# mLSTM output product ahead of the gated unit, head normalisation in its own lane, one output-gate pair by seven products

## The chip, the cores and the metric

One NeuronCore of a Trainium2 chip runs the whole kernel. The metric is the device time of one execution in microseconds (us), shown as the median of several runs; a profiled execution gives the trace.

## The reference

One decoder layer over 1024 tokens and 16 meta tokens, D = 1024, float32. The parts that matter here:

```
p     = h @ w_in + b_in            # u_s5 | q | k | v | o | i | f | g_s5 | g_m
y_s5  = GLU(GELU(S5(u_s5)))        # S5: grouped state-space mixer; GLU by s5_w_glu (512 x 2048)
hm    = HeadNorm(mLSTM(q, k, v, i, f))            # 4 heads, value width 256
y_m   = (sigmoid(o) * hm) @ m_w_out               # 1024 x 1024
mix   = sigmoid(g_s5) * y_s5 + sigmoid(g_m) * y_m
h     = LN(alpha * h + mix @ w_o)
h     = LN(alpha * h + relu(h @ w_up + b_up)^2 @ w_down)
```

HeadNorm subtracts the mean and divides by the standard deviation over each head's 256 values.

## The kernel before, in words

Every large product is done in three matmuls: each operand is split into a high and a low part (`hi`, an fp32r copy made by ScalarE, and `lo`, the remainder made by VectorE), and `mm3` (L262 to L278) adds hi·hi, hi·lo and lo·hi in PSUM. A product with 512 columns and eight blocks of 128 rows is 24 matmuls.

The first half of the kernel is a list of jobs, written out by hand in `ORDER`. `q`, `v`, `u` and `o` jobs are projections of one weight tile each; an `o` job computes the output-gate tile `f` (two halves of 512 positions, eight blocks, three matmuls: 48 matmuls, `o_job`), applies the sigmoid and stores the row to `sig_dr`. An `a` and a `b` job together compute a *pair* of gate tiles by a Strassen scheme, with seven block products instead of eight, 12 matmuls each: `a` does products 1, 3 and 2, and stores weight sums (`gw_dr`) and a partial result (`e_dr`) for later; `b` does 6, 5, 7 and 4, where 4 is done in the next `b` job. For `b` the transformed activations `T` have replaced the activations in `hT_hi` and `hT_lo`. Pairs 0 to 3 are output-gate tiles 0 to 7 (tiles 2p and 2p+1), pairs 4 to 11 the gates g_s5 and g_m. The first three `b` jobs of the list keep their operands in SBUF (`HELD`); the others load them again. The last three `a` jobs are the `TAIL`, whose products are interleaved.

After the `b` jobs come eight `glu` jobs (48 matmuls each), eight `ym` jobs (48 each), and, outside the list, w_o, the up and the down products. Each job's weights are loaded two jobs ahead and split one job ahead (`job.after`).

Everything else runs in *lanes*: Python generators that `pump` advances while `mm3` emits matmuls. A lane's `yield d` lets it rest for d times its `PACE`, on a clock that counts a 512-column matmul as 0.2133 us. `ml` is the mLSTM recurrence, one chunk of 128 positions after the other (`A(c)`, `B(c)`), and with it the head normalisation `N(half, ...)`: a square root on ScalarE, short steps and four scalings on VectorE, eight transposes on TensorE, a copy on ScalarE. `s5c`, `s5` and `s5g` are the S5 tables, batches and GELU rows. `hg` (`hm_gate`) loads normalised rows and sigmoid rows, multiplies and stores them to `hm_dr`; `hmo_load` loads them again and splits them for `ym`, three in slots, five in rows of `hT`. `ah` and `up` prepare w_o and the up product. Loads and stores are issued on SP's queue in program order. The framework (`schedule_with_timeline_sim`) orders the instructions of each engine by a timeline of its own, so instructions of several jobs and lanes mix.

Of the kernel before, what the change touches and what calls it, by code (L numbers as in the profile page):

```python
# [16 lines left out]
D = 1024  # L17
# [20 lines left out]
LN2_1 = 0.693359375  # L38
LN2_2 = math.log(2.0) - LN2_1
MAGIC = 1.5 * 2 ** 23  # L40
ORDER = 'q1 q0 v0 v1 q3 q2 o3 v2 o6 o0 u0 u1 v3 o2 o7 o4 o5 u2 a4 o1 a6 u3 a5 a8 a7 a11 a9 a10 b11 b9 b10 b5 b8 b4 b6 b7'
HMO_AT = 4
HS = 3
HOLD = 3
TF = 1
TFA = 1
TLA = 1
T_UP = 0
REST = 17.25
G_E = [9]  # L50
G_L = [9, 10]
HGD = 1
UPD = 1
TPW = 5.95
S5_START = 'o3'
LANE_AT = {'t_prep': 'q1', 'hm_gate': 'b10', 'ah_scale': 'glu2', 'up_early': 'ym3'}
PACE = {'ml': 0.448, 'cv': 0.104, 's5': 1.05, 's5c': 0.683, 's5g': 2.31, 'ah': 0.834, 'up': 1.036, 'hg': 2.056}
UP = {'ml': 0, 'cv': 0, 's5': 0, 's5c': 0, 's5g': 0, 'ah': 0, 'up': 0, 'hg': 0}
SPLIT_UP = 0
PRE = 3  # L60
UP_AT = (0, 1, 4, 6)
ZD = 1
ML = [1.438, 1.186, 1.852, 10.348]
NL = [0.292, 2.192, 5.096, 3.406]
B5 = [16, 0.1, 0.1, 50]
C5 = [0.84, 0.84, 1.345, 1.05]
K5 = [1.18, 1.0, 8.0, 0.95]
Z5 = [2.284, 1.33, 1.336, 0.283]
D5 = [3.696, 1.28, 1.716, 0.267]
W5 = [5.284, 0.829, 10.595, 0.808]  # L70
Y5 = [0.959, 2.294, 4.502, 2.394]
CV0 = 0
HRA = 0
# [72 lines left out]
def decoder_block(  # L146
# [354 lines left out]
    def mlstm(h):  # L501
# [94 lines left out]
        for c in range(NCH):  # L596
            if c + 1 < NCH:
                A(c + 1)
            yield ML[h]
            B(c)  # L600
            yield ML[h]
            if c == 5:
                yield from N(0, nrm[0])
        yield 1.5
        yield from N(1, nrm[1])

    us_dr = dram.tile([512, 8, NB], F32, name="us_dr")
    ys_dr = dram.tile([4, P, 8, P], F32, name="ys_dr")
# [286 lines left out]
    def s5_batch(b):  # L895
# [71 lines left out]
        nc.sync.dma_start(ys_dr[b].rearrange("p g c -> p (g c)"), Y[:, 0:1024])  # L967
        lanes["s5g"].add(s5_gelu(b))

    def s5_gelu(b):  # L970
        yield 3.0
        yc = slot("s5yc")
        for g in range(8):
            src = ys_dr[b, :, (g % 2) * 4 + g // 2, :].rearrange("(t h) c -> h t c", h=16)
            nc.sync.dma_start(yc[16 * g:16 * g + 16, 0:1024].rearrange("p (t c) -> p t c", t=8), src)
        yield 14.0
        gf = slot("gelf")
        a_.activation(gf[:, 0:1024].rearrange("p (c t) -> p t c", t=8),
                      yc[:, 0:1024].rearrange("p (t c) -> p t c", t=8), AF.Gelu_apprx_tanh)
        hi, lo = slot("gelh", F32R), slot("gell", F32R)  # L980
        a_.activation(hi[:, 0:1024], gf[:, 0:1024], AF.Copy)
        v_.tensor_tensor(lo[:, 0:1024], gf[:, 0:1024], f32(hi[:, 0:1024]), op=OP.subtract)
        GEL[b] = (hi, lo)
        yield 2.6

    HMO = {}

    def hm_gate():
        rs = {}
        for f in range(KT + HGD):  # L990
            if f < KT:
# [12 lines left out]
    def hmo_load():
        rs = {}
        for k in range(KT + 2):
            if k < KT:
                rs[k] = slot("hmr")
                nc.sync.dma_start(rs[k][:, :D], hm_dr[k])
            if k >= 2:  # L1010
                r, q = rs.pop(k - 2), k - 2
                if q < HS:
                    HMO[q] = split_act(r, "hmo")
                else:
                    HMO[q] = hi, lo = hT_hi[:, q, 0:D], hT_lo[:, q, 0:D]
                    a_.activation(hi, r[:, :D], AF.Copy)
                    v_.tensor_tensor(lo, r[:, :D], f32(hi), op=OP.subtract)
            yield 1.2

    def split_act(src, name, n=1024):  # L1020
        hi, lo = slot(name + "h", F32R), slot(name + "l", F32R)
# [16 lines left out]

    MIX, SG, SGM = {}, {}, {}

    def sg_fetch(f):
        SG[f] = slot("sgs")
        nc.sync.dma_start(SG[f][:, :D], sig_dr[KT + f])

    def glu_job(f):
        def run(job):
            if f == 0:
                lanes["s5c"].drain()
                lanes["s5"].drain()
                lanes["s5g"].drain()  # L1050
                lanes["hg"].drain()
                sg_fetch(0)
            if f == HMO_AT:
                lanes["s5"].add(hmo_load())
            if f + 1 < KT:
                sg_fetch(f + 1)
            if f >= KT - 2:
                ms_fetch(f - KT + 2)
            (wh, wl), = job.w
            z2 = slot("z2s")  # L1060
            MIX[f] = SG.pop(f)
# [12 lines left out]
            if f == 0:  # L1074
                for zz in (1, 0):
                    for bi in range(2):
                        part(zz, bi, (0, 1, 2))
            for zz in (1, 0):
                for bi, (c0, c1) in enumerate(HALF):
                    part(zz, bi, (3,) if f == 0 else (0, 1, 2, 3))  # L1080
                    ps = pss[zz, bi]
                    if zz:
                        a_.activation(z2[:, c0:c1], ps, AF.Sigmoid)
                        if bi == 0:
                            job.after()
# [188 lines left out]
    def gb_job(p):  # L1274
        def run(job):
            last = list(GB)
            GB[p] = dict(w=job.w, e=job.w.pop("e") or HELD[p][2])
            if not B_AFT:
                job.after()
            gb_step(p, 6)  # L1280
            if B_AFT:
                job.after()
            gb_step(p, 5)
            for q in last:
                gb_step(q, 4)
# [215 lines left out]
    for w in ORDER.split():  # L1501
# [58 lines left out]
    for i, j in enumerate(jobs):  # L1560
# [610 lines left out]
```

## Time and profile before

| | us |
|---|---|
| median of 3 runs (lowest, highest) | 1501.3 (1501.07, 1501.62) |
| the profiled execution | 1501.45 |
| its span, first to last instruction | 1499.7 |
| TensorE busy | 1483.9 |
| VectorE busy | 1059.4 |
| ScalarE busy | 633.8 |

Busy times are of the profiled execution; matmuls overlap, and their ends are modelled, so busy TensorE time says when the engine had work and not how fast it ran.

### The profile page before, as it was taken

Reading aid. Unit: us, or ns where it says so; the run is one execution under the profiler, and the core shown is the slowest. Engines: PE = TensorE matmul, PEld = TensorE weight load, DVE = VectorE, ACT = ScalarE, POOL = GpSimd, SP = SyncE. Lnnn points to the kernel's source line nnn. Section 1 sums busy time; section 2 is a strip of 40 time slices with the busy share of each in tenths; the row PEclk is TensorE's granted clock in tenths of the full one; section 3 lists DMA queues with packets and bytes.
Section 4 is the critical chain, followed back from the end, with each engine's and each line's share of the span. In section 5 each row is a group of like instructions: output and inputs, shape, how many; then the busy total and the mean of one; then the engine's idle time right before and its main releaser. Section 6 shows DMA issues by size and latency. Waiting matters only on the chain.

```text
span 1499.7 us, 20533 instructions
## 1 busy us (share of the span) xinstructions
PE 1483.9 (99%) x7534; PEld 1253.1 (84%) x7534; DVE 1059.4 (71%) x1920; ACT 633.8 (42%) x1001; POOL 22.4 (1%) x113
## 2 busy tenths in 40 slices
PE   9999999999999999999999999999999999999997
PEld 9999888998888878888888888888888888888886
DVE  8875779686586765674786666566666789657786
ACT  7523544342366554231362244444444624333440
POOL 0000000000000000000000010000000000000000
PEclk9999999999999999999999999999999999999999
DMA  8544035647569699897782267444443997666652
GB/s 333 204 151 137 24 112 201 208 153 254 165 248 315 193 319 385 330 413 272 285 304 85 85 187 258 165 148 151 144 154 125 323 398 250 224 230 229 214 182 99
DMA packets 130516, 324.49 MB, mean 216 GB/s; under 512 B 18336, under 2 KB 32736, under 8 KB 130416
## 3 DMA queue, kind: packets, MB, share of 16 engines
q1 hardware_dynamic: 127392, 312.18, 59.4%
q0 software_dynamic: 3024, 11.01, 2.4%
q8 instruction: 59, 0.97, 0.3%
q14 instruction: 41, 0.34, 0.1%
HBM read 213.33 MB, written 109.81 MB: 215 GB/s over the span
## 4 chain that ended last, share of the span: by engine, by line
PE 82%; DVE 3%; ACT 2%; DMA 1%; issue 1%; SPq 0%; DVEq 0%; ACTq 0%
PE mm L276 20%; PE mm L274 20%; PE mm L275 20%; PE sd L276 6%; PE sd L275 6%; PE sd L274 6%; PE pn L542 1%; PE pn L543 1%; PE pu L546 1%; PE ln L1652 0%; DMA s5RS<-rr_dr 0%; PE s5y L962 0%; DVE s5w L935 0%; PE pS L532 0%; DMA s5yc<-ys_dr 0%
## 5 line engine op out<-in xcount | busy, mean ns | idle before, releaser
L274 PE MATMUL mm<-hT_hi,whi 128*128 128x512 f32 (+3 forms) x400 | 146.6, 367 | 0.0
L275 PE MATMUL mm<-hT_lo,whi 128*128 128x512 f32 (+3 forms) x400 | 146.2, 365 | 0.0
L276 PE MATMUL mm<-hT_hi,wlo 128*128 128x512 f32 (+3 forms) x400 | 145.5, 365 | 0.3 <-DVE wlo L255 0.3
L276 PE MATMUL sd<-dwh,dal 128*128 128x512 f32 (+1 forms) x256 | 99.1, 387 | 0.0
L275 PE MATMUL sd<-dwl,dah 128*128 128x512 f32 (+1 forms) x256 | 99.0, 387 | 0.0
L274 PE MATMUL sd<-dwh,dah 128*128 128x512 f32 (+1 forms) x256 | 98.6, 386 | 0.0
L1861 ACT ACTIVATE dah<-da 128x1024 fp32r<-128x1024 f32 x56 | 58.7, 1052 | 85.4 <-DMA da<-act_dr 36.2
L1865 ACT ACTIVATE dwh<-wdr 128x1024 fp32r<-128x1024 f32 x56 | 58.9, 1054 | 81.8 <-DVE wdr L1847 23.8
L276 PEld LDWEIGHTS mm<-hT_hi,wlo 128*128 128x128 f32 x400 | 75.3, 188 | 10.5 <-issue 0.7
L274 PEld LDWEIGHTS mm<-hT_hi,whi 128*128 128x128 f32 x400 | 75.3, 188 | 9.5 <-issue 0.5
L275 PEld LDWEIGHTS mm<-hT_lo,whi 128*128 128x128 f32 x400 | 75.3, 188 | 9.1 <-issue 0.3
L1862 DVE TENSOR_TENSOR dal<-da,dah 128x1024 fp32r<-128x1024 f32 x56 | 68.1, 1220 | 17.5 <-ACT dah L1861 17.4
L274 PE MATMUL mm<-dwh,dah 128*128 128x512 f32 (+1 forms) x208 | 79.8, 384 | 0.0
L276 PE MATMUL mm<-dwh,dal 128*128 128x512 f32 (+1 forms) x208 | 79.8, 385 | 0.0
L275 PE MATMUL mm<-dwl,dah 128*128 128x512 f32 (+1 forms) x208 | 79.7, 385 | 0.0
L274 PE MATMUL mm<-hT_hi,gmwh 128*128 128x512 f32 x192 | 76.9, 401 | 0.2 <-DVE gme L1255 0.2
L1866 DVE TENSOR_TENSOR dwl<-wdr,dwh 128x1024 fp32r<-128x1024 f32 x56 | 68.2, 1220 | 11.9 <-ACT dwh L1865 11.3
L275 PE MATMUL mm<-hT_lo,gmwh 128*128 128x512 f32 x192 | 75.7, 394 | 0.0
L276 PE MATMUL mm<-hT_hi,gmwl 128*128 128x512 f32 x192 | 74.6, 395 | 0.0
L274 PE MATMUL mm<-whi,hT_hi 128*128 128x256 f32 (+1 forms) x256 | 74.0, 290 | 0.0
L275 PE MATMUL mm<-wlo,hT_hi 128*128 128x256 f32 (+1 forms) x256 | 73.6, 288 | 0.0
L276 PE MATMUL mm<-whi,hT_lo 128*128 128x256 f32 (+1 forms) x256 | 73.2, 287 | 0.0
(468 smaller groups left out, 3843.7 us busy)
## 6 DMA issues: line engine op xcount, KB each, us to landing
da<-act_dr SPq DMA_DIRECT2D x56, 512.0 KB
wdr<-in_wdn_dram SPq DMA_DIRECT2D x56, 512.0 KB
wraw<-in_wf_dram SPq DMA_DIRECT2D x36, 512.0 KB
wur<-in_wup_dram SPq DMA_DIRECT2D x32, 512.0 KB
act_dr<-upy SPq DMA_DIRECT2D x64, 256.0 KB
wu_dr<-wpre SPq DMA_DIRECT2D x21, 512.0 KB
wpre<-wu_dr POOLq DMA_DIRECT2D x21, 512.0 KB, 5.3
act_dr<-upx SPq DMA_DIRECT2D x32, 256.0 KB
```

Source lines behind the costliest of these rows:

```text
L274: t_.matmul(ps, ah, bh, start=(i == 0 and part[0]), stop=False, skip_group_check=skip)
L275: t_.matmul(ps, ah, bl, start=False, stop=False, skip_group_check=skip)
L276: t_.matmul(ps, al, bh, start=False, stop=(i == n - 1 and part[1]), skip_group_check=skip)
L542: t_.matmul(pn[:, :258], qi[:, c0:c0 + n], Cs[c][:, :258], start=True, stop=False)
L543: t_.matmul(pn[:, :258], sws[c], vt[c][:, :258], start=False, stop=True)
L546: t_.matmul(pu[:, :258], kws[c][:n], vt[c][:n, :258], start=True, stop=True)
L1861: a_.activation(ah[:, :D], a[:, :D], AF.Copy)
L1862: v_.tensor_tensor(alo[:, :D], a[:, :D], f32(ah[:, :D]), op=OP.subtract)
L1865: a_.activation(wh, raw[i], AF.Copy)
L1866: v_.tensor_tensor(wl, raw[i], f32(wh), op=OP.subtract)
```

## The change

- `ORDER` is new. Jobs `o6` and `o7` are gone; pair 3 (`a3`, `b3`) computes these two gate tiles. `a3` stands after `v2`, where `o6` was; `b3` stands sixth among the nine `b` jobs. `a9 a5 a10` are the tail. Tiles 6 and 7 count as done (`OD`) after product 4 of pair 3, in the job after `b3`.
- The `ym` jobs come ahead of the `glu` jobs. `ym` stores sigmoid times product to `mix_dr`; `glu` loads it and adds. `hmo_load` has a lane `hm` that starts at the last `b` job and waits for gated rows and for free rows of `hT`. Up to three GELU rows go into rows of `hT`.
- `N` is added to a lane `hn` instead of being run inside `ml`, its first half after chunk 4 instead of 5. `HRA = 1` does two of four scalings on ScalarE.
- Paces, start points, priorities (`UP`, `T_UP`) and rests have new values.

```diff
-ORDER = 'q1 q0 v0 v1 q3 q2 o3 v2 o6 o0 u0 u1 v3 o2 o7 o4 o5 u2 a4 o1 a6 u3 a5 a8 a7 a11 a9 a10 b11 b9 b10 b5 b8 b4 b6 b7'
-HMO_AT = 4
+ORDER = 'q1 q0 v0 v1 q3 q2 o3 v2 a3 o0 u0 u1 v3 o2 o4 o5 u2 o1 a4 a6 a7 u3 a11 a8 a9 a5 a10 b9 b10 b5 b4 b3 b6 b8 b11 b7'
 HS = 3
+GH = 3
-T_UP = 0
-REST = 17.25
-G_E = [9]
-G_L = [9, 10]
+T_UP = 100
+REST = 11.83
+G_E = [5, 10]
+G_L = [5]
-LANE_AT = {'t_prep': 'q1', 'hm_gate': 'b10', 'ah_scale': 'glu2', 'up_early': 'ym3'}
-PACE = {'ml': 0.448, 'cv': 0.104, 's5': 1.05, 's5c': 0.683, 's5g': 2.31, 'ah': 0.834, 'up': 1.036, 'hg': 2.056}
+LANE_AT = {'t_prep': 'q0', 'hm_gate': 'a8', 'hmo': 'b7', 'ah_scale': 'ym5', 'up_early': 'glu3'}
+PACE = {'ml': 0.56, 'cv': 0.104, 's5': 1.103, 's5c': 0.683, 's5g': 3.512, 'ah': 1.602, 'up': 1.036, 'hg': 1.92, 'hn': 1.0, 'hm': 0.66}
+UP = {'ml': 10, 'cv': 0, 's5': 0, 's5c': 0, 's5g': 0, 'ah': 0, 'up': 0, 'hg': 0, 'hn': 0, 'hm': 0}
-ML = [1.438, 1.186, 1.852, 10.348]
-NL = [0.292, 2.192, 5.096, 3.406]
+ML = [1.912, 1.186, 1.815, 10.865]
+NL = [0.584, 3.726, 10.192, 11.252]
...
-HRA = 0
+HRA = 1
@@ mlstm @@
-            if c == 5:
-                yield from N(0, nrm[0])
-        yield 1.5
-        yield from N(1, nrm[1])
+            if c == 4:
+                lanes["hn"].add(N(0, nrm[0]))
+        lanes["hn"].add(N(1, nrm[1]))
@@ s5_gelu @@
-        GEL[b] = (hi, lo)
+        if 1 in ROWS and len(GROW) < GH:
+            GROW.append(KT - 1 - len(GROW))
+            GEL[b] = split_row(gf, GROW[-1])
+        else:
+            GEL[b] = split_act(gf, "gel")
@@ hm_gate @@
                 nc.sync.dma_start(hm_dr[f - HGD], a[:, :D])
+                GATED.add(f - HGD)
@@ hmo_load @@
             if k < KT:
+                while k not in GATED:
+                    yield 0.5
...
+                    while (q - HS) // 4 not in ROWS:
+                        yield 0.5
+                    HMO[q] = split_row(r, q - HS)
+    def split_row(src, row):
+        hi, lo = hT_hi[:, row, 0:D], hT_lo[:, row, 0:D]
+        a_.activation(hi, src[:, :D], AF.Copy)
+        v_.tensor_tensor(lo, src[:, :D], f32(hi), op=OP.subtract)
+        return hi, lo
@@ glu_job @@
-                        v_.tensor_tensor(MIX[f][:, c0:c1], z2[:, c0:c1], MIX[f][:, c0:c1], op=OP.mult)
-                        if bi == 1:
-                            nc.sync.dma_start(mix_dr[f], MIX.pop(f)[:, :D])
+                        v_.tensor_tensor(z2[:, c0:c1], z2[:, c0:c1], SG[f][:, c0:c1], op=OP.mult)
+                        v_.tensor_tensor(MIX[f][:, c0:c1], MIX[f][:, c0:c1], z2[:, c0:c1], op=OP.add)
@@ gb_job @@
             gb_step(p, 5)
+            if p == B_END:
+                ROWS.add(0)
...
             if p == B_END:
                 gb_flush()
+                ROWS.add(1)
@@ ym_job @@
-            lanes["s5"].drain()
+            if f == 0:
+                for n in ("cv", "ml", "hn", "hg", "hm"):
+                    lanes[n].drain()
+            if f + 1 < KT:
+                sm_fetch(f + 1)
+            if f >= KT - 2:
+                ms_fetch(f - KT + 2)
...
-                v_.tensor_tensor(MIX[f][:, c0:c1], MIX[f][:, c0:c1], SGM[f][:, c0:c1], op=OP.add)
...
+            nc.sync.dma_start(mix_dr[f], SGM.pop(f)[:, :D])
```

## Rows read from the trace of the kernel before

**Rows 1.** The page: span, busy time by engine, the chain that ended last.
```profile
span 1499.7 us, 20533 instructions
PE 1483.9 (99%) x7534; PEld 1253.1 (84%) x7534; DVE 1059.4 (71%) x1920; ACT 633.8 (42%) x1001; POOL 22.4 (1%) x113
PE 82%; DVE 3%; ACT 2%; DMA 1%; issue 1%; SPq 0%; DVEq 0%; ACTq 0%
```
**Rows 2.** Busy time by stretches (stretch, length, engines with counts, clock, DMA share, GB/s).
```profile
0.00:100.00 100.00, 97.10 (x782) 94.47 (x783) 83.26 (x178) 54.77 (x113) 3.33 (x42) 1.00 0.67 247
100.00:550.00 450.00, 445.37 (x2608) 391.28 (x2607) 323.47 (x794) 208.25 (x330) 7.33 (x49) 1.00 0.57 188
200.00:250.00 50.00, 49.23 (x319) 44.79 (x319) 46.56 (x155) 21.59 (x34) 2.05 (x17) 1.00 0.37 121
450.00:550.00 100.00, 99.25 (x467) 81.49 (x466) 71.39 (x113) 61.43 (x83) 0.95 (x1) 1.00 0.81 271
550.00:1450.00 900.00, 900.00 (x3923) 731.65 (x3922) 615.47 (x861) 368.36 (x551) 11.27 (x21) 1.00 0.66 234
1450.00:1499.70 49.70, 41.39 (x226) 35.73 (x224) 37.17 (x89) 2.38 (x8) 0.52 (x1) 0.96 0.23 85
```
**Rows 3.** Timeline of TensorE in a full stretch: start, length, instruction.
```profile
581.73 0.39 PE L276 MATMUL mm<-hT_hi,gmwl 128*128 128x512 f32 x1
...
586.84 0.39 PE L274 MATMUL mm<-gelh,whi 128*128 128x512 f32 x1
```
**Rows 4.** Waits of TensorE from 100 to 560 us: total, times, longest.
```profile
PE pt L586 <- DVE hraw L579: 1.8, 1, 1.8
PE pS L532 <- ACT kw L529: 0.7, 2, 0.5
PE s5y L962 <- DVE s5w L947: 0.6, 1, 0.6
PE pS L532 <- ACT hmF L587: 0.5, 1, 0.5
PE pn L542 <- DVE hmv L566: 0.3, 1, 0.3
PE mm L276 <- DVE wlo L255: 0.3, 1, 0.3
PE mm L274 <- DVE gme L1255: 0.2, 1, 0.2
```
**Rows 5.** Groups by line: busy us, mean ns, idle before, releaser.
```profile
L1462 DVE TENSOR_TENSOR wus<-wus,wraw 128x512 f32<-128x512 f32 x8 | 5.5, 687 | 0.2
L1023 DVE TENSOR_TENSOR gmwl<-wraw,gmwh 128x1024 fp32r<-128x1024 f32 x7 | 8.6, 1222 | 4.2 <-ACT gmwh L1022 4.2
L1022 ACT ACTIVATE gmwh<-wraw 128x1024 fp32r<-128x1024 f32 x8 | 8.5, 1062 | 4.3 <-DMA gw_dr<-wus 3.2 <-DMA gw_dr<-wraw 1.1
L564 ACT ACTIVATE hraw<-pn,dd 128x256 f32<-128x256 f32 x32 | 15.1, 473 | 71.2 <-DVE dd L563 64.2 <-PE pn L543 3.2 <-DVE cpre L356 2.6
L579 DVE TENSOR_SCALAR hraw<-hraw,hmv,hny 128x256 f32<-128x256 f32 x32 | 11.0, 408 | 0.0
```
**Rows 6.** Busy time by stretches: ten microseconds with the DMA engines full.
```profile
560.00:570.00 10.00, 10.00 (x45) 8.13 (x44) 6.27 (x7) 4.84 (x6) 0.00 (x0) 1.00 1.03 399
```
**Rows 7.** Timeline around the wait of the transposes.
```profile
148.67 1.28 ACT L207 ACT_TABLE_LOAD   x1
149.96 0.30 ACT L207 ACTIVATE hny<-hmv,eps_t 128x4 f32<-128x4 f32 x1
151.64 1.38 DVE L579 TENSOR_SCALAR hraw<-hraw,hmv,hny 128x256 f32<-128x256 f32 x4
152.10 0.44 PE L586 MATMUL pt<-ident,hraw 128*128 128x128 f32 x2 [1.81 <-DVE hraw L579]
```
**Rows 8.** SP's timeline: the last load of a sigmoid row for the gating.
```profile
591.75 0.66 SPq L996 DMA_DIRECT2D hgo<-sig_dr  x1
```
**Rows 9.** The gating multiply by its tile: duration, first and last start.
```profile
L1000 DVE TENSOR_TENSOR hgr<-hgr,hgo x8: 1214/1226/1227, 544.8 to 601.4; 128x1024 f32<-128x1024 f32 x8
```

More of the change, by code (lines that the diff above doesn't have):

```diff
@@ L47 @@
 TLA = 1
-T_UP = 0
-REST = 17.25
-G_E = [9]
-G_L = [9, 10]
+T_UP = 100
+REST = 11.83
+G_E = [5, 10]
+G_L = [5]
 HGD = 1
 UPD = 1
-TPW = 5.95
+TPW = 5.29
 S5_START = 'o3'
-LANE_AT = {'t_prep': 'q1', 'hm_gate': 'b10', 'ah_scale': 'glu2', 'up_early': 'ym3'}
-PACE = {'ml': 0.448, 'cv': 0.104, 's5': 1.05, 's5c': 0.683, 's5g': 2.31, 'ah': 0.834, 'up': 1.036, 'hg': 2.056}
-UP = {'ml': 0, 'cv': 0, 's5': 0, 's5c': 0, 's5g': 0, 'ah': 0, 'up': 0, 'hg': 0}
+LANE_AT = {'t_prep': 'q0', 'hm_gate': 'a8', 'hmo': 'b7', 'ah_scale': 'ym5', 'up_early': 'glu3'}
+PACE = {'ml': 0.56, 'cv': 0.104, 's5': 1.103, 's5c': 0.683, 's5g': 3.512, 'ah': 1.602, 'up': 1.036, 'hg': 1.92, 'hn': 1.0, 'hm': 0.66}
+UP = {'ml': 10, 'cv': 0, 's5': 0, 's5c': 0, 's5g': 0, 'ah': 0, 'up': 0, 'hg': 0, 'hn': 0, 'hm': 0}
 SPLIT_UP = 0
@@ L62 @@
 ZD = 1
-ML = [1.438, 1.186, 1.852, 10.348]
-NL = [0.292, 2.192, 5.096, 3.406]
+ML = [1.912, 1.186, 1.815, 10.865]
+NL = [0.584, 3.726, 10.192, 11.252]
 B5 = [16, 0.1, 0.1, 50]
-C5 = [0.84, 0.84, 1.345, 1.05]
-K5 = [1.18, 1.0, 8.0, 0.95]
-Z5 = [2.284, 1.33, 1.336, 0.283]
+C5 = [0.84, 0.798, 1.345, 4.956]
+K5 = [1.652, 1.0, 8.0, 0.475]
+Z5 = [2.284, 1.264, 0.394, 0.269]
 D5 = [3.696, 1.28, 1.716, 0.267]
-W5 = [5.284, 0.829, 10.595, 0.808]
-Y5 = [0.959, 2.294, 4.502, 2.394]
+W5 = [5.284, 0.829, 15.575, 0.848]
+Y5 = [0.792, 1.657, 4.502, 6.57]
 CV0 = 0
-HRA = 0
+HRA = 1
 A_AFT = 0
@@ L968, in s5_batch @@
         lanes["s5g"].add(s5_gelu(b))
+    ROWS, GROW = set(), []
     def s5_gelu(b):
@@ L979, in s5_gelu @@
                       yc[:, 0:1024].rearrange("p (t c) -> p t c", t=8), AF.Gelu_apprx_tanh)
-        hi, lo = slot("gelh", F32R), slot("gell", F32R)
-        a_.activation(hi[:, 0:1024], gf[:, 0:1024], AF.Copy)
-        v_.tensor_tensor(lo[:, 0:1024], gf[:, 0:1024], f32(hi[:, 0:1024]), op=OP.subtract)
-        GEL[b] = (hi, lo)
+        if 1 in ROWS and len(GROW) < GH:
[3 more added lines that the diff above has]
+            GEL[b] = split_act(gf, "gel")
         yield 2.6
-    HMO = {}
+    HMO, GATED = {}, set()
     def hm_gate():
@@ L1014, in hmo_load @@
                 else:
-                    HMO[q] = hi, lo = hT_hi[:, q, 0:D], hT_lo[:, q, 0:D]
-                    a_.activation(hi, r[:, :D], AF.Copy)
-                    v_.tensor_tensor(lo, r[:, :D], f32(hi), op=OP.subtract)
+                    while (q - HS) // 4 not in ROWS:
+                        yield 0.5
+                    HMO[q] = split_row(r, q - HS)
             yield 1.2
+    def split_row(src, row):
[3 more added lines that the diff above has]
+        return hi, lo
     def split_act(src, name, n=1024):
@@ L1039, in decoder_block, with sm_fetch @@
     MIX, SG, SGM = {}, {}, {}
-    def sg_fetch(f):
-        SG[f] = slot("sgs")
-        nc.sync.dma_start(SG[f][:, :D], sig_dr[KT + f])
+    def sm_fetch(f):
+        SGM[f] = slot("sgmr")
+        nc.sync.dma_start(SGM[f][:, :D], sig_dr[2 * KT + f])
     def glu_job(f):
@@ L1050, in run @@
                 lanes["s5g"].drain()
[L1051 to L1058, printed above, removed]
+            if f + 2 < KT:
+                ms_fetch(f + 2)
             (wh, wl), = job.w
             z2 = slot("z2s")
-            MIX[f] = SG.pop(f)
             pss = {}
@@ L1087, in run @@
                         v_.tensor_tensor(z2[:, c0:c1], ps, z2[:, c0:c1], op=OP.mult)
-                        v_.tensor_tensor(MIX[f][:, c0:c1], z2[:, c0:c1], MIX[f][:, c0:c1], op=OP.mult)
-                        if bi == 1:
-                            nc.sync.dma_start(mix_dr[f], MIX.pop(f)[:, :D])
+                        v_.tensor_tensor(z2[:, c0:c1], z2[:, c0:c1], SG[f][:, c0:c1], op=OP.mult)
+                        v_.tensor_tensor(MIX[f][:, c0:c1], MIX[f][:, c0:c1], z2[:, c0:c1], op=OP.add)
+            SG.pop(f)
         all_jobs.append(Job([(wglu[f].rearrange("p k z f -> p (k z f)"), 1024)], run))
@@ L1292, in ms_fetch @@
     def ms_fetch(f):
-        MIX[f], SGM[f] = slot("mixr"), slot("sgmr")
+        MIX[f], SG[f] = slot("mixr"), slot("sgs")
         nc.sync.dma_start(MIX[f][:, :D], mix_dr[f])
-        nc.sync.dma_start(SGM[f][:, :D], sig_dr[2 * KT + f])
+        nc.sync.dma_start(SG[f][:, :D], sig_dr[KT + f])
     def ym_job(f):
         def run(job):
-            lanes["s5"].drain()
-            if f + 2 < KT:
-                ms_fetch(f + 2)
+            if f == 0:
+                for n in ("cv", "ml", "hn", "hg", "hm"):
+                    lanes[n].drain()
+                sm_fetch(0)
+            if f + 1 < KT:
+                sm_fetch(f + 1)
+            if f >= KT - 2:
+                ms_fetch(f - KT + 2)
             (wh, wl), = job.w
@@ L1308, in run @@
                 v_.tensor_tensor(SGM[f][:, c0:c1], ps, SGM[f][:, c0:c1], op=OP.mult)
-                v_.tensor_tensor(MIX[f][:, c0:c1], MIX[f][:, c0:c1], SGM[f][:, c0:c1], op=OP.add)
                 if bi == 0:
                     job.after()
-            SGM.pop(f)
+            nc.sync.dma_start(mix_dr[f], SGM.pop(f)[:, :D])
         all_jobs.append(Job([(wmo[f].rearrange("p k f -> p (k f)"), 1024)], run))
@@ L1517, in decoder_block @@
     for f in range(KT):
+        ym_job(f)
+        all_jobs[-1].tag = f"ym{f}"
+    for f in range(KT):
         glu_job(f)
         all_jobs[-1].tag = f"glu{f}" if f else "glu"
-    for f in range(KT):
-        ym_job(f)
-        all_jobs[-1].tag = f"ym{f}"
     for i, j in enumerate(all_jobs):
@@ L1572, in decoder_block @@
             lanes["s5c"].add(s5_tables())
-        for lane, name, gen in (("ah", "t_prep", t_prep), ("hg", "hm_gate", hm_gate), ("ah", "ah_scale", ah_scale),
-                                ("up", "up_early", up_early)):
+        for lane, name, gen in (("ah", "t_prep", t_prep), ("hg", "hm_gate", hm_gate), ("hm", "hmo", hmo_load),
+                                ("ah", "ah_scale", ah_scale), ("up", "up_early", up_early)):
             if j.tag == LANE_AT[name]:
@@ L1577, in decoder_block @@
         if j.tag == "glu":
-            for n in ("cv", "ml", "s5c", "s5", "s5g"):
+            for n in ("cv", "ml", "hn", "s5c", "s5", "s5g"):
                 lanes[n].drain()
```

## The prediction

> **What bounds the kernel now.** I read the page first: TensorE is busy 99% of a span of 1499.7 us, VectorE 71%, ScalarE 42%, and the chain that ended last lies 82% on TensorE [rows 1]. A busy TensorE need not run at its best pace, so the second view is the busy time by stretches: where TensorE is idle, and at what clock [rows 2]. The first 100 us, which the edits leave alone but for a few paces, lose 2.9 us. From 100 to 550 us 450 - 445.37 = 4.63 us are idle. From 550 to 1450 there is nothing to lose: 900.00 of 900. The last stretch loses 8.3 us, the closing normalisation. The granted clock is 1.00, the 2.4 GHz level, in every stretch but that last one. The third view is the pace inside a full stretch: from the matmul at 581.73 to that at 586.84 us lie 22 starts, 5.11 us, so a 512-column matmul takes 0.232 us [rows 3]. A "product" below is 12 of these: 2.79 us. Fourth, the waits of TensorE: seven kinds, all before 550 us, 4.4 us together; the largest, 1.8 us, is the transposes of the head normalisation waiting for the normalised rows [rows 4].
>
> So the kernel is a queue of matmuls that is never empty after 550 us. A change gives what it takes out of that queue, plus what it takes from the 4.63 us of waits, less waits of its own. Nothing else that it moves can show.
>
> **Part 1: one output-gate pair by seven products.** Two plain gate jobs (o6, o7) are each 2 halves x 8 blocks x 3 matmuls = 48, together 96. Pair 3 (a3 and b3) is 7 products x 12 = 84. Twelve matmuls fewer, at 0.232 us: **-2.79 us**. All have 512 columns before and after, and by the full stretches of [rows 2] none of that time is hidden behind anything.
>
> The rule for this price is in the Trainium skill, "TensorE: Matmul & The Clock Gate", section "Wait — 56ns, not 53.3ns?": a warm matmul costs its columns at 2.4 GHz plus about 2.5 ns, 215.7 ns for 512. The trace says 232, so that rule would give -2.59 us; the row's price stands in the sum.
>
> The pair costs VectorE more. In a3: four sums of 0.69 us, one split of 1.22 us and one half split, taken like a sum at 0.69 [rows 5], 4.7 us where o6 needs one split of 1.22: +3.4 us. In b3: two splits and four adds, each taken like a sum, 5.2 us where o7 had 1.2. TensorE hides this unless VectorE runs late. b3 falls into the b jobs, after 450 us; VectorE is busy 71 of 100 us there [rows 2], which hides 4 us: nothing. But a3 stands where o6 stood, and the stretch 200 to 250 has VectorE busy 46.56 of 50 us [rows 2]. What is late there is the next weight split, for which a matmul waits (0.3 us such a wait is in [rows 4]). Bounds 0 and the whole 3.4 us; jobs are prepared one ahead, and most of the normalisation work of that stretch is spread elsewhere, so I take +0.5.
>
> Traffic: the pair stores 1.5 MB (two weight sums, one partial result) and loads them again, 3.0 MB more, 7.5 us of transfer at the 399 GB/s of a stretch with the DMA engines full [rows 6]. No matmul waits for a DMA in [rows 4]; it is nothing, unless the last rows of the mLSTM path are late (rival 3).
>
> **Part 2: normalisation in its own lane, mLSTM slower, half of the scaling on ScalarE.** [Rows 7] show the wait of 1.81 us. The square root needs a table load on ScalarE (148.67, 1.28 us), then the root, five short VectorE steps, four scalings of 1.38 us in all, and the transposes start at 152.10, 1.81 us after TensorE was through with its last matmul. Before, the normalisation stands in the mLSTM lane, and for head 0 its steps are 0.292 x 0.448 = 0.13 lane-us apart. After, twice 0.584 x 1.0: 0.91 lane-us more between chunk and transposes. Lane time counts 0.2133 us where the matmul takes 0.232 (x1.088), so 1.0 us. Two of four scalings go to ScalarE; the nearest row there is 0.473 us against 0.408 [rows 5], so the four take about 0.95 instead of 1.38 us: 0.4 less. Together 1.4 of the 1.8 us, and the split queued behind the scalings (0.3) follows. The other waits of the lane (kw 0.7, hmF 0.5, hmv 0.3) come from chunks of head 0 every 2 x 1.438 x 0.448 = 1.29 lane-us; after, 2 x 1.912 x 0.56 = 2.14. I let half of these 1.5 us go. Sum: -1.4 - 0.3 - 0.8 = **-2.5 us**; bounds 0 (the lane is late in other places) and all 4.63. Sixteen scalings on ScalarE, 7.6 us, fall into a stretch where it is busy 208 of 450 us [rows 2].
>
> The Trainium skill, "ScalarE: Activation LUTs", section "What ACT_TABLE_LOAD costs", puts a drain of about 1.38 us behind each 1.28-us load. By it this chain would be 1.4 us longer and part 2 worth only 1.1 us; here the root starts 1.29 us after the load began [rows 7], so no drain is added.
>
> **Part 3: ym ahead of the gated unit.** Matmuls: the same 48 per job in both. VectorE: each half has four operations before (multiply, multiply; multiply, add) and four after, one and three. DMAs: the same loads and stores of mix_dr and the two sigmoid rows, in swapped jobs. Nothing in the sum. What moves is who must be ready. The gated unit gains a stage (8 x 48 x 0.232 = 89 us) of time for the S5 rows. The ym product loses as much: it needs all eight gated rows, which now must stand at the end of the last b job. Price nothing, the cover worked out in rival 3. At its end, the last job now has three VectorE steps of 0.69 us behind it instead of two, but its first half is through 12 matmuls (2.8 us) before the end, and w_o reads that block last, 21 matmuls (4.9 us) into its first row: covered. Five hT rows freed late become three.
>
> **Part 4: order, paces, early or late splits.** These move instructions between engines that have idle time; their worth is in part 2. The stage of w_o, up and down keeps its instructions and its start relative to the second of the swapped stages.
>
> **Sum**, against the profiled execution's 1501.45 us: -2.79 (matmuls) -2.5 (waits) +0.5 (a3) = -4.8, so 1496.65; the median of the runs lies 0.15 below that execution: **1496.5 us**. A measurement of this kernel tells 0.2%, 3.0 us, from no change, so "faster" begins at 1498.3 and "slower" at 1504.3.
>
> **Rivals.**
>
> 1. The waits only change place. [Rows 7] show a chain of 3.4 us from the table load to the transposes, and the scheduler that orders the engines put it flush behind a chunk once; it can do so for another head, or a3 is late by 2 to 3 us. For: VectorE at 93% from 200 to 250 [rows 2]. Against: more time between the steps. Only the matmuls count: 1501.3 - 2.8 = 1498.5, up to 1501 with a late a3.
> 2. All waits go: 1501.3 - 2.79 - 4.63 = 1493.9. Against: two of them (s5w 0.6, gme 0.2) are not touched.
> 3. The other side: ym waits for its last rows. Gate tiles 6 and 7 are now finished in the job after b3, with 14 products left (39.0 us), the eighth row being needed 21 matmuls later (43.9 us). In that time hm_gate fetches and multiplies rows 6 and 7: 23.0 lane-us, 25.1 us; the fetch of row 7 follows eight steps of 0.79 after the start of b7, at 31.1. The nearest row for a landing: loads issued at 591.75, the last multiply at 601.4 [rows 8, 9], 10 us with the DMA engines full. Then 1.06 + 1.22 us of splits [rows 5]: 43.4, half a microsecond before the need. If the gate's load, its store and the load after it take 10 us each, it is 25.1 + 1.7 + 10 + 10 + 2.3 = 49.1, a wait of 5.2 us, and with no early wait gone the time is 1501.3 - 2.8 + 5.2 = 1503.7. It decides from 2.8 us of wait on, i.e. from 9.2 us a landing. For: the eight rows are 4.2 MB, 10.5 us at 399 GB/s, in the last b job. Against: the b jobs' own loads have ended by then.
>
> For that ceiling, the Trainium skill ("DMA: Bandwidth & Descriptors", "Where 436 GB/s comes from") names 435 GB/s for the ports and about 358 for HBM; the row has 399 [rows 6]. An estimate by 358 makes it 11.7 us for the eight rows, 1.2 us later.
>
> **Numbers.** Forecast (1494.5 to 1498.3): 0.46. Rival 1 (1498.3 to 1501.5): 0.28. Rival 2 (below 1494.5): 0.11. Rival 3: 0.15, half of it above 1504.3. Faster: 0.46 + 0.11 = 0.57; same: 0.28 + 0.07 = 0.35; slower: 0.08. Range 1493.8 to 1502.5: from all waits gone to rival 3 at four fifths of its wait; about 2 in 10 lie outside.
>
> **What would show it.** Right: 12 matmuls of 512 columns fewer; idle time of TensorE from 100 to 550 near 2.5 us with no transposes waiting over 0.5 us; none between the last b job and the first w_o row. Part 1 is wrong if a3's matmuls wait for VectorE by more than 1 us; part 2 if the transposes still wait over a microsecond; part 3 if TensorE waits for hmo or hT rows at the start of ym, or for MIX or hT rows at w_o. A wait in the up or down stage would mean that something I called unmoved has moved.

## The result and the profile after

The changed kernel takes 1507.7 us (median of 6 runs, 1506.56 to 1510.97) against 1501.46 (6 runs, 1501.07 to 1501.86) measured beside it: ratio 1.0044, 95% interval 1.0031 to 1.0057. It is slower by 6.2 us; the forecast was 1496.5 us, and its range ended at 1502.5.

The page of the changed kernel, the lines that answer to [rows 1]:

```profile
span 1506.1 us, 20548 instructions
PE 1484.5 (99%) x7522; PEld 1251.7 (83%) x7522; DVE 1061.1 (70%) x1914; ACT 644.9 (43%) x1022; POOL 22.1 (1%) x113
PEclk9999999999999999999989999999999999999999
```

Twelve matmuls fewer (7534 to 7522), yet the span is 6.4 us longer, and one of forty slices of the span has a TensorE clock (PEclk, in tenths) below the others. Its busy time by stretches, the columns as in [rows 2]:

```profile
0.00:100.00 100.00, 96.00 (x780) 93.37 (x781) 80.50 (x173) 56.53 (x115) 3.34 (x42) 1.00 0.62 226
100.00:550.00 450.00, 446.50 (x2614) 391.65 (x2613) 333.88 (x799) 218.08 (x348) 6.93 (x49) 1.00 0.65 218
...
750.00:800.00 50.00, 44.21 (x175) 34.84 (x174) 38.35 (x98) 28.74 (x85) 2.30 (x4) 0.90 0.62 232
```

From 100 to 550 us TensorE is idle for 3.50 us instead of 4.63. TensorE is busy without a gap from 550 to 750 and from 800 to 1450. The stretch from 750 to 800, which lay in the full part of [rows 2], is now neither full nor at full clock. The same fifty microseconds of the kernel before:

```profile
750.00:800.00 50.00, 50.00 (x218) 40.63 (x217) 39.01 (x105) 25.27 (x80) 2.29 (x4) 1.00 0.62 227
```

175 matmuls instead of 218: 43 x 0.232 = 10.0 us lost here, more than the whole difference. The waits of TensorE from 100 to 800 us in the changed kernel (total, times, longest) name the place:

```profile
PE mm L274 <- ACT hT_hi L1607: 5.2, 1, 5.2
PE s5z L907 <- DVE s5Z L915: 1.5, 1, 1.5
PE pS L532 <- ACT hraw L564: 0.8, 1, 0.8
PE mm L275 <- DVE hT_lo L1608: 0.6, 1, 0.6
PE pS L532 <- ACT kw L529: 0.5, 1, 0.5
PE mm L274 <- DVE gmx L1266: 0.4, 1, 0.4
```

The transposes' wait of [rows 4] (pt, 1.8) is gone, and with it hmF, hmv, wlo and s5w. New are s5Z and hraw, 2.3 us, and the two on hT_hi and hT_lo, 5.8 us: the split rows of w_o, which stand in the buffer that held the activations. TensorE's timeline there:

```profile
769.27 0.40 PE L276 MATMUL mm<-hT_hi,wlo 128*128 128x512 f32 x1
774.87 2.50 PE L274 MATMUL mm<-hT_hi,mxh 128*128 128x512 f32 x5 [5.20 <-ACT hT_hi L1607]
777.95 0.80 PE L275 MATMUL mm<-hT_lo,mxh 128*128 128x512 f32 x1 [0.59 <-DVE hT_lo L1608]
778.55 0.63 PE L276 MATMUL mm<-hT_hi,mxl 128*128 128x512 f32 x1
...
783.67 0.46 PE L276 MATMUL mm<-hT_hi,mxl 128*128 128x512 f32 x1
```

The gated unit ends at 769.7 (774.87 less the wait); the product with w_o should follow at once. Before, it did: the stage ended, and w_o began, at 772.59. So up to here the change was 2.9 us ahead. From 778.55 to 783.67 twelve matmuls start in 5.12 us, 0.427 us each instead of 0.232 [rows 3]. The windows of that stretch show why (the last three columns are clock, DMA share and GB/s):

```profile
769.70:773.00 3.30, 0.00 (x0) 0.00 (x0) 3.30 (x14) 3.30 (x18) 0.00 (x0) 1.00 1.03 415
773.60:783.80 10.20, 8.35 (x19) 6.09 (x20) 10.20 (x29) 10.04 (x29) 0.00 (x0) 0.50 0.91 364
783.80:794.00 10.20, 10.20 (x46) 8.24 (x45) 7.71 (x20) 4.20 (x9) 0.00 (x0) 1.00 0.17 53
```

TensorE does nothing for 5.2 us; from 773.6 the granted clock is 0.50 (1.2 GHz), for 10.2 us; in this time 19 matmuls start, in the next 10.2 us 46. The wait of 5.8 us so costs 10.0. "TensorE: Matmul & The Clock Gate" of the Trainium skill, section "Wait — 56ns, not 53.3ns?", gives a matmul of 512 columns 426.7 ns at that level; the trace agrees, with 0.427 us.

Where the split rows come from. While the second stage runs, the lane `up` adds and subtracts blocks of the up weights and stores the results to `wu_dr` (the early up sums, 21 stores). In the program all of these stand ahead of the loads of w_o. The section on the kernel before says that SP issues in program order; here it does not, since the framework reorders SP's instructions too. SP's timeline in the kernel before:

```profile
751.94 3.07 SPq L1595 DMA_DIRECT2D woraw<-in_wo_dram  x2
755.10 1.50 SPq L1489 DMA_DIRECT2D wu_dr<-wpre  x3
756.65 0.90 SPq L1595 DMA_DIRECT2D woraw<-in_wo_dram  x2
757.59 0.43 SPq L1489 DMA_DIRECT2D wu_dr<-wpre  x1
758.83 8.46 SPq L1595 DMA_DIRECT2D woraw<-in_wo_dram  x4
```

SP's timeline in the changed kernel:

```profile
744.42 13.84 SPq L1500 DMA_DIRECT2D wu_dr<-wpre  x9
758.36 13.13 SPq L1606 DMA_DIRECT2D woraw<-in_wo_dram  x8
```

Before, the first load was issued 20.7 us ahead of w_o's start and four of the loads stood ahead of the last store; after, 11.3 us ahead and behind all of them. A line of SP's waits from 740 to 775 us, in the kernel before:

```profile
SPq L1595 <- DMA wu_dr<-wpre: 6.0, 3, 2.3
```

In the changed kernel:

```profile
SPq L1606 <- DMA wu_dr<-wpre: 9.8, 6, 2.9
```

There six of the eight loads wait for a store of the sums to land. Loads, sums and rows all live in the 30 buffers that `slot` hands out (the ring), and a buffer is free when its store is through. ScalarE's timeline in the kernel before:

```profile
758.83 1.06 ACT L1596 ACTIVATE hT_hi<-woraw 128x1024 fp32r<-128x1024 f32 x1 [4.84 <-DMA woraw<-in_wo_dram]
762.38 1.06 ACT L1596 ACTIVATE hT_hi<-woraw 128x1024 fp32r<-128x1024 f32 x1 [2.49 <-DMA woraw<-in_wo_dram]
763.35 2.90 ACT L1609 ACTIVATE mxh<-mixr 128x128 fp32r<-128x128 f32 x14
```

ScalarE's timeline in the changed kernel:

```profile
764.63 1.50 ACT L1620 ACTIVATE mxh<-mixr 128x128 fp32r<-128x128 f32 x7
767.36 6.51 ACT L1620 ACTIVATE mxh<-mixr 128x128 fp32r<-128x128 f32 x32 [1.23 <-DMA wu_dr<-wpre]
773.76 1.05 ACT L1607 ACTIVATE hT_hi<-woraw 128x1024 fp32r<-128x1024 f32 x1
```

Before, two split copies of w_o stand ahead of the mix copies (the `hi` copies of the mix, 128x128 each); after, 39 mix copies stand ahead of the first, which starts the moment they end. The load came 6.4 us later, the copy 14.9. Before, ScalarE waited for the first load until 6.9 us after its issue; by that (an estimate) it was there at 765.3 in the changed kernel, 8.5 us before its copy. So what TensorE waits for at the first row is, by this, the copy's place on ScalarE. No run moved the copy without the load.

The sum of the traces, in span: the second of the swapped stages ends 2.9 us earlier; from there to the first up matmul (867.77 before, 874.80 after) are 105.1 us instead of 95.2, +9.9; the rest of the kernel is 0.6 us shorter. Together +6.4.

### The profile page after: what moved, and what is told of

Its sections match the earlier page's. It is cut to its first block, busy times and chain, and to the rows that moved or that the text cites. A ratio compares the mean times of both kernels' runs of the same rounds, so it can differ in the third digit from the quotient of the medians.

```text
span 1506.1 us, 20548 instructions
## 1 busy us (share of the span) xinstructions
PE 1484.5 (99%) x7522; PEld 1251.7 (83%) x7522; DVE 1061.1 (70%) x1914; ACT 644.9 (43%) x1022; POOL 22.1 (1%) x113
## 4 chain that ended last, share of the span: by engine, by line
PE 93%; DVE 3%; DMA 2%; ACT 2%; issue 1%; SPq 0%; DVEq 0%; ACTq 0%
PE mm L276 22%; PE mm L275 22%; PE mm L274 22%; PE sd L275 6%; PE sd L274 6%; PE sd L276 6%; PE mm L270 2%; PE mm L309 1%; PE pn L542 1%; PE pn L543 1%; PE pu L546 1%; DMA wu_dr<-wpre 1%; DMA wraw<-in_wf_dram 1%; PE ln L1663 0%; PE pt L586 0%
## 5 line engine op out<-in xcount | busy, mean ns | idle before, releaser
L274 PE MATMUL mm<-hT_hi,whi 128*128 128x512 f32 (+3 forms) x432 | 158.9, 369 | 0.0
L275 PE MATMUL mm<-hT_lo,whi 128*128 128x512 f32 (+3 forms) x432 | 158.3, 366 | 0.0
L276 PE MATMUL mm<-hT_hi,wlo 128*128 128x512 f32 (+3 forms) x432 | 158.1, 367 | 0.0
L274 PEld LDWEIGHTS mm<-hT_hi,whi 128*128 128x128 f32 x432 | 81.3, 188 | 11.0 <-issue 0.7
L275 PEld LDWEIGHTS mm<-hT_lo,whi 128*128 128x128 f32 x432 | 81.3, 188 | 10.9 <-issue 0.5
L276 PEld LDWEIGHTS mm<-hT_hi,wlo 128*128 128x128 f32 x432 | 81.2, 188 | 10.5
L274 PE MATMUL mm<-hT_hi,gmwh 128*128 128x512 f32 x216 | 86.8, 404 | 0.4 <-DVE gmx L1266 0.4
L275 PE MATMUL mm<-hT_lo,gmwh 128*128 128x512 f32 x216 | 85.1, 394 | 0.0
L276 PE MATMUL mm<-hT_hi,gmwl 128*128 128x512 f32 x216 | 84.9, 397 | 0.0
L1877 DVE TENSOR_TENSOR dwl<-wdr,dwh 128x1024 fp32r<-128x1024 f32 x56 | 68.2, 1219 | 11.1 <-ACT dwh L1876 10.5
```

The source lines that it names most:

```text
L274: t_.matmul(ps, ah, bh, start=(i == 0 and part[0]), stop=False, skip_group_check=skip)
L275: t_.matmul(ps, ah, bl, start=False, stop=False, skip_group_check=skip)
L276: t_.matmul(ps, al, bh, start=False, stop=(i == n - 1 and part[1]), skip_group_check=skip)
L1877: v_.tensor_tensor(wl, raw[i], f32(wh), op=OP.subtract)
```

## The experiments

Theory A: the start of w_o alone separates the changed kernel from its forecast, because the rows of w_o are loaded and copied too late. Rivals: the scaling of the residual (ah_scale), now at `ym5`, crowds it (B); the GELU rows in hT keep it back (C); the three VectorE steps behind the last gated job make the mixed rows late (D); it is the swap, or the pair, or the lane, that costs by itself.

**The scaling early, in a lane of its own.**

```diff
-'ah_scale': 'ym5'
+'ah_scale': 'ym2'          # lane 'as', pace 0.834
```

> The changed kernel, with ah_scale in a lane of its own, started at the third job of its stage (ym2) and paced 0.834, as in the kernel before. Theory A (TensorE waits at w_o because w_o's first rows are loaded and copied too late: their loads stand behind the 21 stores of up_early on SP's queue and their copies behind 39 mix copies on ScalarE): nothing changes in that order, so the wait of about 5 us at w_o and the half clock after it stay, 1506 to 1509 us. Rival B (the later and slower ah_scale holds slots and DMA time and so pushes up_early and the w_o loads back): the wait goes and the time falls by about 10 us, to 1497 to 1498.

1507.71 us, ratio 1.0043 (1.0026 to 1.0060). The largest wait of TensorE:

```profile
PE mm L274 <- ACT hT_hi L1607: 5.3, 1, 5.3
```

The loads are issued from 758.4 to 771.2 as in the change. Rival B falls.

**No GELU rows in hT.**

```diff
-GH = 3
+GH = 0
```

> The changed kernel with GH = 0: no GELU rows in hT, so no row of hT is read until the end of the last gated job. Theory A: w_o waits for its first row, not for a row that a GELU row held, so the wait stays, though it may shorten by the 8 mix copies fewer that stand ahead of the first w_o copy (8 x 0.2 us): 1504 to 1508 us. Rival C (GELU rows in hT hold up w_o's rows): the wait goes, 1497 to 1499.

1508.64 us, ratio 1.0050 (1.0035 to 1.0064). The wait on hT_hi is 5.9 us, on hT_lo 0.7; the six operands held in slots instead put the loads at 767.7 to 778.1, 9 us later than in the change. Rival C falls. Three of the loads stand ahead of the last store here, as before, and the wait is there all the same; the first load is issued 3.5 us ahead of the need. So a place between the stores does not help where the lead is short.

**Four rows of w_o loaded and split in the second gated job.**

```diff
+        if j.tag == "glu1":
+            for k in range(WO_EARLY):      # 4
+                wo_row_load(k)
...
-    for k in range(KT):
+    for k in range(WO_EARLY, KT):
```

> The changed kernel, with the first four rows of w_o loaded and split in the second gated job (glu1), nothing else moved. Theory A: the wait at w_o goes (under 1 us is left), the clock stays at its upper level through the stage, and the time falls by the 5.8 us of wait and some 4.5 us of half clock: 1497 to 1498.5. Rival D (the three VectorE steps behind the last gated job make the mixed rows late): the wait stays, now on a mix copy, 1505 to 1508.

1498.24 us (10 runs, 1497.52 to 1500.38), ratio 0.9983 (0.9974 to 0.9992). The stretch of the loss:

```profile
750.00:800.00 50.00, 50.00 (x217) 40.50 (x216) 40.71 (x112) 25.25 (x83) 2.29 (x4) 1.00 0.55 200
```

The largest wait left from 100 to 800 us is 1.1 us, on s5Z. Nothing waits at w_o, the clock is full, 9.5 us come back. Rival D falls, since the three steps are unmoved. Theory A holds, as far as early rows go.

**The early up sums started two gated jobs sooner.** This edit touches no load of w_o, only what stands ahead of them on SP's queue and in the ring.

```diff
-'up_early': 'glu3'
+'up_early': 'glu1'
```

> The changed kernel with up_early started two jobs earlier (glu1 in place of glu3). Theory A: the 21 stores are through some 15 to 20 us earlier, w_o's loads are issued before the last gated job, and the wait at w_o shrinks to under 2 us: 1497 to 1501. Rival D: no change, 1506 to 1509.

1498.86 us (10 runs), ratio 0.9985 (0.9975 to 0.9994). SP's timeline with this edit:

```profile
738.67 5.93 SPq L1500 DMA_DIRECT2D wu_dr<-wpre  x5
744.65 5.98 SPq L1606 DMA_DIRECT2D woraw<-in_wo_dram  x8
```

The loads still follow the last store, 14 us sooner, with a lead of 23.9 us; none waits for a store of the sums to land. The first split copy is at 766.53, behind 14 mix copies instead of 39, and no wait is left at w_o. Two edits that share an earlier load, and with it an earlier copy, remove the same loss.

**One mix row less held.** In the changed kernel the gated unit fetches stored rows two jobs ahead; here one ahead.

```diff
-            if f + 2 < KT:
-                ms_fetch(f + 2)
+            if f + 1 < KT:
+                ms_fetch(f + 1)
```

> The gated unit fetches each stored row of the mix one job ahead instead of two, so that one 4-KB row less is held while the early rows of up are summed. If it is places in the ring that keep the loads of w_o back, these are issued earlier than 758.4 us, the wait at w_o's start falls from 5.8 us to under 4 and the time to 1503 to 1506. If the order of the loads behind the stores of up's sums on SP's queue alone sets them, nothing changes: wait 5 to 6 us, 10 us at the lower clock, 1506 to 1509.

1507.85 us (1507.42 to 1509.22), ratio 1.0045 (1.0031 to 1.0058). The first load is issued at 758.8, no earlier, and the wait is longer. ScalarE's timeline with this edit:

```profile
776.49 1.50 ACT L1620 ACTIVATE mxh<-mixr 128x128 fp32r<-128x128 f32 x7 [1.02 <-DVE z2s L1092]
777.90 1.99 ACT L1607 ACTIVATE hT_hi<-woraw 128x1024 fp32r<-128x1024 f32 x2
```

The stretch of the lower clock, columns as above; the wait on hT_hi is 8.8 us:

```profile
773.00:783.20 10.20, 4.21 (x10) 3.34 (x11) 10.10 (x36) 9.18 (x34) 0.00 (x0) 0.50 1.01 407
```

The first copy of w_o now stands behind 46 mix copies, whose rows come a job later. So one place more in the ring does not bring the loads forward, though six of them still wait for a store to land; the expectation of the queue's order had the time right, the wait wrong. The wait on hT_hi is 3.6 us longer than in the changed kernel, the time is not: the clock is at 0.50 for 10.2 us in both, and here 6 of these pass in the wait.

**The change without the swap.** The gated unit first, as before; the order, pair, lane and S5 paces of the change. The edit also sets SPLIT_UP, the priority of the weight splits, to 100, which is 0 in both kernels.

```diff
-SPLIT_UP = 0
+SPLIT_UP = 100
-LANE_AT = {..., 'hmo': 'b7', 'ah_scale': 'ym5', 'up_early': 'glu3'}
+LANE_AT = {..., 'ah_scale': 'glu5', 'up_early': 'ym3'}
...
```

> Everything of the change but the swap: the kernel before (gated unit first, then ym) with the new order, pair 3, normalisation lane, paces, priorities; hm_gate starts at a8, ah_scale at the sixth job of its stage (glu5), up_early at ym3, as in the changed kernel's places. Theory A in its wider form (the swap puts the gated unit's ScalarE and VectorE work into the stage in which up_early and w_o's rows are prepared, and so makes these late): the wait at w_o is gone or under 2 us, 1497 to 1500 us. Rival E (the order and paces make them late, the swap is innocent): a wait of 4 to 6 us at w_o and half clock after it, 1505 to 1508.

1506.27 us (10 runs, 1503.5 to 1508.15), ratio 1.0026 (1.0017 to 1.0036); the profiled execution took 1504.42. Its waits on w_o's rows and at the start of the gated unit:

```profile
PE mm L275 <- DVE hT_lo L1597: 1.5, 2, 1.2
PE mm L274 <- ACT gelh L980: 1.3, 1, 1.3
PE mm L274 <- ACT hT_hi L1596: 0.8, 1, 0.8
PE mm L275 <- DVE gell L981: 0.5, 1, 0.5
```

At w_o 2.3 us instead of 5.8 (5.2 + 0.6); in exchange the gated unit waits 1.8 us for its S5 rows, which the swap had given 89 us more. The first load has a lead of 13.3 us, and behind the wait of 1.2 us the clock is at 0.50 for 3.4 us. Neither side of the expectation came: the swap is not shown to be the whole of the wait, and it is worth something elsewhere. What SPLIT_UP adds was not taken apart.

**The swap alone.** The swap with the lanes it needs and their paces; order, plain o6 and o7, normalisation and the paces of the S5 and mLSTM lanes as before.

```diff
-ORDER = '... v2 a3 o0 u0 u1 v3 o2 o4 ...'
+ORDER = '... v2 o6 o0 u0 u1 v3 o2 o7 o4 ...'     # that of before
...
-            if c == 4:
-                lanes["hn"].add(N(0, nrm[0]))
-        lanes["hn"].add(N(1, nrm[1]))
+            if c == 5:
+                yield from N(0, nrm[0])
+        yield 1.5
+        yield from N(1, nrm[1])
```

> The swap of the two stages alone, with what it needs (gating and loads of hmo in their lanes, both late lanes started as in the change); order, split pair, normalisation and paces of the S5 and mLSTM lanes as before. If the swap with its late sums is enough for the wait at w_o: 4 to 6 us of wait there and 10 us at the lower clock, 1501.3 + 5.8 + 4.2 = about 1511 with before's early waits. If the wait needs the rest of the change too: under 2 us at w_o, 1501 to 1504.

1529.54 us (1527.09 to 1532.14), ratio 1.0188 (1.0174 to 1.0202). The two largest waits of TensorE from 100 to 800 us:

```profile
PE mm L274 <- ACT gmwh L1034: 7.1, 3, 4.2
PE mm L274 <- ACT hT_hi L1608: 5.9, 1, 5.9
```

The wait at w_o is there without the pair and the lane: the swap, in this order, is enough for it. The first load has a lead of 2.9 us. From the end of the gated unit (788.6) to the first up matmul (894.44) are 105.9 us, 10.7 more than before. The other 18 us were not expected (the forecast of this run was about 1511): the largest waits there are on the pairs' reloaded weights (gmwh, 7.1), which the order of the change doesn't have; the rest was not taken apart.

**The pair alone.** Before, with `a3` and `b3` in place of `o6` and `o7`.

```diff
-... v2 o6 o0 u0 u1 v3 o2 o7 o4 ... b5 b8 b4 b6 b7
+... v2 a3 o0 u0 u1 v3 o2 o4 ... b5 b8 b3 b4 b6 b7
```

> The kernel before with pair 3 alone: o6 becomes a3, o7 is dropped, b3 stands sixth among the b jobs; nothing else. By 12 matmuls of 0.232 us the time falls by 2.8 us, to 1498.4 us, if VectorE's 3.4 us more at a3 are hidden; by a late a3 it falls by 0 to 2 us only, with a wait of TensorE on a3's weights between 210 and 250 us.

1512.44 us (1510.29 to 1514.03), ratio 1.0073 (1.0058 to 1.0088). The largest waits of TensorE:

```profile
PE mm L274 <- ACT gmo L1170: 4.9, 2, 4.5
PE pu L546 <- DVE s5Z L916: 2.2, 1, 2.2
PE pt L586 <- DVE hraw L579: 1.8, 1, 1.8
```

The matmuls are gone (7522), but the waits between 100 and 800 us grow from 4.4 to about 12.4; the largest is at 491 us, not at a3 where it was looked for, and 13.6 us run at clock 0.50 behind these three, by the windows:

```profile
153.00:156.40 3.40, 3.40 (x17) 3.22 (x16) 3.33 (x6) 2.35 (x3) 0.00 (x0) 0.50 0.31 82
422.60:426.00 3.40, 3.23 (x10) 2.98 (x11) 3.37 (x7) 1.58 (x4) 0.00 (x0) 0.50 0.22 80
490.90:497.70 6.80, 6.21 (x15) 4.91 (x16) 4.27 (x5) 5.42 (x8) 0.95 (x1) 0.50 0.98 283
```

**The lane alone.** Before, with `N` in lane `hn`, the change's pace, priority and rests of `ml` and `N`, and two scalings on ScalarE.

```diff
-            if c == 5:
-                yield from N(0, nrm[0])
-        yield 1.5
-        yield from N(1, nrm[1])
+            if c == 4:
+                lanes["hn"].add(N(0, nrm[0]))
+        lanes["hn"].add(N(1, nrm[1]))
...
-HRA = 0
+HRA = 1
```

> The kernel before with the normalisation lane alone: N in lane hn, its pace 1.0, the new NL and ML, ml paced 0.56 with priority 10, half of the scalings on ScalarE. By the prediction's second part the waits of TensorE from 100 to 550 us fall from 4.6 to about 2 us, with no wait of the transposes over 0.5 us: 1498.5 to 1500 us. By the rival (the waits change place) other waits take their room: 1500.5 to 1502.

1508.64 us (1506.08 to 1509.83), ratio 1.0047 (1.0032 to 1.0062). The largest waits:

```profile
PE pt L586 <- ACT hraw L577: 2.6, 2, 2.2
PE mm L276 <- DVE wlo L255: 1.9, 1, 1.9
PE mm L274 <- ACT whi L254: 1.0, 1, 1.0
```

The transposes wait again, at another head (198 us), for a scaling that now stands on ScalarE. Rival 1's sentence on the scheduler that puts the chain flush behind a chunk "for another head" is what happens here. The sum of the waits grows from 4.4 to 7.4 us, and two stretches of 3.4 us run at clock 0.50; both ends of the expectation were too low.

**The pace of the S5 lane as before, with the early rows.**

```diff
-Z5 = [2.284, 1.264, 0.394, 0.269]
+Z5 = [2.284, 1.264, 1.336, 0.269]
```

> The changed kernel with the first four w_o rows early (as in the run before), and one S5 pace back at its old value: Z5 of batch 2 is 1.336 in place of 0.394, so the four state products of that batch come 1.5 instead of 0.4 lane-us apart. If this pace made the new wait of the S5 product on VectorE (0.8 to 2.5 us near 404 us), the wait goes and the time is about 1 us below that of the run with early rows alone, 1497 to 1498; if not, it stays.

1498.92 us (10 runs, 1497.44 to 1501.21), ratio 0.9983 (0.9973 to 0.9992): no different from the early rows alone. The wait for s5Z stays (1.67 us); that pace does not make it.

**Both repairs together.** The four early rows, and:

```diff
-'up_early': 'glu3'
+'up_early': 'glu1'
```

> Four rows of w_o early and the lane of up's sums started at the second gated job as well. The theory that the start of w_o is all that separates the changed kernel from its forecast has nothing left to give here: 1497.5 to 1499.5, like either edit alone, with no wait at w_o and idle time of TensorE from 100 to 550 us of 3 to 4.5 us. The rival, that the remaining early waits come from work pushed together by the late start of up's sums, would give under 1496.5.

1498.52 us (11 runs, 1496.85 to 1501.35), ratio 0.9982 (0.9973 to 0.9991), idle time from 100 to 550 us 450 - 446.05 = 3.95 us. Like either alone: nothing of the loss is left at w_o. The simplest version that beats both kernels, the one before by 0.15%, is the change with `up_early` at `glu1`.

## Why the prediction was wrong

- **Part 1, -2.79 us: right.** 7522 matmuls for 7534, at 0.232 us where the clock is full. The a3 term (+0.5) did not come: no weight of a3 is waited for, and VectorE is busy 39.19 us instead of 46.56 from 200 to 250 us. But the pair by itself, in the order of before, costs 11 us (1512.44), which the part did not contain.
- **Part 2, -2.5 us: right in kind, mis-sized.** The five waits named (pt, hmF, hmv, wlo, part of kw) went, 3.1 us; s5w (0.6) and gme (0.2), which I had left alone, went too; s5Z (1.5), hraw (0.8) and gmx (0.4) came. The idle time from 100 to 550 us fell by 1.1, not 2.5. That waits partly change place was rival 1; by itself the lane makes them grow (1508.64).
- **The first 100 us** lost 4.0 us, not 2.9: at 11.1 us the first products wait 1.21 us for ScalarE's hf. In the experiments on the changed kernel, with the same code there, this wait is 0.41 us in one and in no list in two others, so it is not put down to the change.
- **Part 3, start of ym: right.** No matmul waits for hmo or hT rows there; rival 3's 5.2 us did not come. The S5 rows of the gated unit came in time; without the swap, at the new paces, they don't. (In rival 3 the fetch at 31.1 us follows seven steps of 0.79, not eight; the sum stands.)
- **Part 3's end and Part 4: the failed step.** "At its end, ... covered" looked at the three VectorE steps behind the last gated job, and they are covered. "The stage of w_o, up and down keeps its instructions and its start relative to the second of the swapped stages" is where it broke. I priced the hT rows and the mix block and did not ask where the eight loads of w_o and their copies stand on SP's and ScalarE's queues. Before, the first two copies stood ahead of the mix copies; the row of this, and the time from the load to the need (20.7 us), could have been read. With the stages swapped, the stores of the up sums run just as far into the second stage, the first load has 11.3 us of lead instead of 20.7, and the first copy falls behind 39 others: 5.8 us. My own list of signs named it: a wait for hT rows at w_o.
- **The price of a wait.** I counted a wait at its length. Behind one of 5.2 us the clock fell to 0.50, and 5.8 us cost 10.0. All waits in the trace of before were under 2 us and no clock of 0.50 followed them, so nothing there gave the price; the forecast had no bound for it.

With the failed step repaired the sum is near: 1498.24 to 1498.86 us, on the border of the forecast (to 1498.3) and rival 1 (from 1498.3), 2.3 to 2.9 us below before, about the twelve matmuls; most of what is missing to 1496.5 is part 2's shortfall of 1.4. The chance that the prediction gave to times above 1504.3 came true by luck: it stood on rival 3's wait for the rows of ym, which did not come.

What stays open: why w_o's loads come so late although the sums' lane starts at the same job of the second stage. The scaling is not it (one experiment). The ring has a part: six of the loads wait for a store to land, and six operands more in it put them 9 us later; but one row less held moved nothing. The traces show one difference more: the first copy of a sum runs at 706.85 us before and at 720.22 after, though the last store goes out at 757.6 and 757.9. From 700 to 758 us of the changed kernel ScalarE waits for TensorE's gated products, with copies of the sums behind them in its queue:

```profile
ACT z2s L1087 <- PE mm L276: 29.9, 7, 7.7
```

Before, ym stood there, and ScalarE waited for TensorE once in that stretch, until 705.89, ahead of its first copy of a sum. One of these waits, 6.49 us, ends at 750.30; the next copy of a sum, its VectorE remainder and its store follow at 751.75, 753.02 and 753.74, and SP issues nothing for 6.1 us. But with the sums two jobs sooner ScalarE waits there too, 20.4 us, and nothing is lost. Which of these sets the loads' place in the order that the scheduler computes, no run took apart.

## What to carry to other kernels

When two stages are swapped, walk through the queues at the next stage's start as well: who issues its loads, behind what, and behind which copies its first operand stands; the lead of each load over its need is a row of the trace. Parts of a change to such an interleaved kernel don't add: pair, lane and swap alone cost 11, 7 and 28 us, together in the order of the change 6, and with one lane's start mended they gain 2.3. Price a wait of TensorE of several microseconds with the slow stretch behind it, not at its length.

## What the runs showed of the hardware

- The stretch at 1.2 GHz was 10.2 us long after waits of 5.2, 5.3, 5.9 and 8.8 us alike, and for as long as TensorE stood idle in it the clock cost nothing: a wait of 8.8 us and one of 5.2 came to nearly the same time (1507.85 and 1507.7 us; 106.0 and 105.1 us from the end of the gated unit to the first up matmul).
- A wait of 4.45 us was followed by 6.8 us at 0.50 in the kernel with the pair alone, one of 4.19 us by 3.4 us in the kernel with the swap alone.
- Shorter waits don't decide it by their length: 1.81 us on the same transposes left the clock full before and was followed by 3.4 us at 0.50 in the kernel with the pair alone; 2.07 us on s5Z left it full with one mix row less, 2.15 us on it did not with the early scaling.
